# Rotary embedding of half a head: how the cosine and sine tables come into 128 partitions

## The chip, the cores and the metric

The kernel runs on one core of a Trainium2 chip. The time is device microseconds of one execution. Before the change it is 161.78 us, the median of three runs (161.61 to 161.86). A profile of one more execution has a span of 159.5 us from its first to its last instruction.

## What is computed

```
x: (16, 512, 16, 64) float32        batch, position, head, dimension
cos, sin: (512, 32) float32         position, half of the dimension

x1, x2 = x[..., :32], x[..., 32:]
first  = x1[..., :16] * cos[..., :16] - x1[..., 16:] * sin[..., :16]
second = x1[..., :16] * sin[..., :16] + x1[..., 16:] * cos[..., :16]
out    = concatenate([first, second, x2], axis=-1)
```

Only the first 32 of each head's 64 elements are turned; the other 32 pass through. Of each table's row, only the first 16 of 32 elements are used, and they serve all batches and heads. x and the output are 33.55 MB each, a table is 64 KB.

## The kernel before, in words

**Tiles.** x is read as one long array of rows, a row being one batch and position (16 heads of 64 elements, 4 KB). Four tiles (T = 4) of 128 partitions hold 16 rows (K = 16) in each partition, 64 KB a partition and 8.4 MB a tile. The buffer `ring` (line 45) holds three tiles, so tile 3 takes the place of tile 0. Since 16 rows of one batch follow each other in a partition, 512 positions fill 32 partitions (PB = 32), and the same pattern of positions repeats in each of the four groups of 32 partitions (REP = 4).

**Tables.** `table` (line 49) holds, for each partition, its 16 rows of cosine and of sine, the 16 used elements written twice in a row so that one multiply covers both halves of x1. So the four groups of 32 partitions hold the same content. It comes about in these steps:

- Line 61: DVE clears the used half of `stage`, in all 128 partitions.
- Lines 62 to 64: POOL issues one DMA for each table. Row j of 32 (16 positions, 2 KB) goes to partition 4j. The first of them waits for the clearing.
- Line 73: one stream shuffle on DVE. Within each group of 32 partitions, it brings the 8 rows that arrived there to 8 neighbouring places (repeated four times), in `spun`.
- Lines 78 to 80: four copies on DVE gather the groups' rows into partitions 0 to 31 of `packed`.
- Lines 82 to 86: four copies on DVE, one for each group of 32 partitions, write `table` from `packed`, each element twice.

**Loads, work and stores.** The functions `load` and `store` (lines 54 to 58) issue one DMA each, on SP's queue if nothing else is said. SP first issues the loads of tile 0, tile 1 and the second half of tile 2 (lines 65 to 67); they wait for nothing. `rotate(t, lo, hi)` (lines 90 to 103) does a part of a tile on DVE with four operations in place: x1 times sine into `b_t`, which lies in PSUM (line 96), x1 times cosine (97), a subtraction (98) and an addition (101). Tiles are done in halves of 8 rows, tile 2 in parts of 8, 5 and 3.

The order of the work is written by hand. After tile 0 is turned, SP issues its store, the load of the first half of tile 2, and the load of tile 3, which has to wait for the store of tile 0. The store of tile 1 is held back by a dependence written by hand (line 118) until the addition of the 5-row part of tile 2 is done. The store of tile 2 goes out on POOL's queue (line 116), the other stores on SP's.

Of the kernel before, what the change touches and what calls it, by code (L numbers as in the profile page):

```python
# [1 line left out]

# [4 lines left out]


@with_exitstack
def kernel(  # L10
    ctx: ExitStack,
    tc: tile.TileContext,
    x: bass.AP,
    cos: bass.AP,
    sin: bass.AP,
    out: bass.AP,
):
    nc = tc.nc
    fp32 = mybir.dt.float32
    P = 128  # L20
    B, S, H, D = x.shape
    Q = D // 4
    HF = D // 2

    K = 16
    T = B * S // (P * K)
    PB = S // K
    REP = P // PB  # L30
    R = H * D
    NS = 3
    KC = K // 2
    KM = 5

    xf = x.rearrange("b s h d -> (b s h d)").rearrange("(t p f) -> t p f", t=T, p=P)
    of = out.rearrange("b s h d -> (b s h d)").rearrange("(t p f) -> t p f", t=T, p=P)
    cosf = cos.rearrange("(p k) j -> p (k j)", k=K)
    sinf = sin.rearrange("(p k) j -> p (k j)", k=K)

    const_pool = ctx.enter_context(tc.tile_pool(name="const", bufs=1))
    b_pool = ctx.enter_context(tc.tile_pool(name="bp", bufs=1, space=bass.MemoryType.PSUM))


    ring = const_pool.tile([P, NS, K, H, D], fp32)
    stage = const_pool.tile([P, 2, K, HF], fp32)
    spun = const_pool.tile([P, 2 * K, Q], fp32)
    packed = const_pool.tile([PB, 2 * K, Q], fp32)
    table = const_pool.tile([P, 2, K, 2, Q], fp32)

    def rows(t, lo, hi):
        return ring[:, t % NS, lo:hi].rearrange("p k h d -> p (k h d)")

    def load(t, lo=0, hi=K):
        return nc.sync.dma_start(out=rows(t, lo, hi), in_=xf[t, :, lo * R : hi * R])

    def store(t, lo=0, hi=K, queue=nc.sync):
        return queue.dma_start(out=of[t, :, lo * R : hi * R], in_=rows(t, lo, hi))  # L58


    nc.vector.memset(stage[:, :, :, 0:Q], 0.0)  # L61
    spread = stage.rearrange("(j b) t k i -> j b t (k i)", b=REP)
    nc.gpsimd.dma_start(out=spread[:, 0, 0], in_=cosf)  # L63
    nc.gpsimd.dma_start(out=spread[:, 0, 1], in_=sinf)  # L64
    load(0)
    load(1)
    load(2, KC, K)

    PQ = PB // REP
    nc.vector.stream_shuffle(  # L73
        out=spun[:],
        in_=stage.rearrange("p t k j -> p (t k) j")[:, :, 0:Q],
        mask=[j % PQ * REP for j in range(PB)],
    )
    for q in reversed(range(REP)):
        n = PQ * (q + 1)
        nc.vector.tensor_copy(out=packed[0:n], in_=spun[q * PB : q * PB + n])  # L80

    for r in range(REP):
        nc.vector.tensor_copy(  # L83
            out=table[r * PB : (r + 1) * PB].rearrange("p t k c j -> p (t k) c j"),
            in_=packed.unsqueeze(2).to_broadcast((PB, 2 * K, 2, Q)),
        )
    C = table[:, 0].rearrange("p k c j -> p k (c j)")
    Sn = table[:, 1].rearrange("p k c j -> p k (c j)")

    def rotate(t, lo, hi):  # L90
        x1 = ring[:, t % NS, lo:hi, :, 0:HF]
        c = C[:, lo:hi].unsqueeze(2).to_broadcast((P, hi - lo, H, HF))
        s = Sn[:, lo:hi].unsqueeze(2).to_broadcast((P, hi - lo, H, HF))
        b_full = b_pool.tile([P, KC, H, HF], fp32, name="b_t")
        b_t = b_full[:, 0 : hi - lo]
        nc.vector.tensor_mul(out=b_t, in0=x1, in1=s)  # L96
        nc.vector.tensor_mul(out=x1, in0=x1, in1=c)  # L97
        nc.vector.tensor_sub(  # L98
            out=x1[:, :, :, 0:Q], in0=x1[:, :, :, 0:Q], in1=b_t[:, :, :, Q:HF]
        )  # L100
        return nc.vector.tensor_add(  # L101
            out=x1[:, :, :, Q:HF], in0=x1[:, :, :, Q:HF], in1=b_t[:, :, :, 0:Q]
        )

    rotate(0, 0, KC)
    rotate(0, KC, K)
    store(0)
    load(2, 0, KC)
    load(3)
    rotate(1, 0, KC)  # L110
    rotate(1, KC, K)
    behind_loads = store(1)
    rotate(2, KC, K)
    near = rotate(2, 0, KM)
    rotate(2, KM, KC)
    store(2, queue=nc.gpsimd)

    tc.add_manual_dep(
        behind_loads.ins,
        near.ins.name,  # L120
        mybir.DependencyInfo(mybir.DependencyClass.Sync, mybir.DependencyReason.DATA),
        reason="the store follows the loads at the DMA engines",
    )
    rotate(3, 0, KC)
    rotate(3, KC, K)
    store(3)


# [1 line left out]
_INS = ['x', 'cos', 'sin']  # L130
_OUTS = [((16, 512, 16, 64), 'float32')]


# [23 lines left out]
```

## Time and profile before

| | |
|---|---|
| Median of three runs | 161.78 us |
| Span of the profiled execution | 159.5 us |
| DVE busy | 112.9 us, 47 instructions |
| Moved by DMA | 67.24 MB, 422 GB/s over the span |
| Load of tile 0: issue, landing | 0.74 us, 22.94 us |
| DVE's first multiply starts | 23.03 us |
| DVE's last addition ends | 131.2 us |
| Issues of the stores of tiles 0, 1, 2, 3 | 49.92, 98.90, 104.62, 131.2 us |
| Landing of the last store, from its issue | 27.4 us |
| Cosine table: issue to landing | 9.0 us |
| Sine table: issue to landing | 13.3 us |

The span begins with the first instruction of the program and ends with the last; the time of a run has 2.3 us around it. The 16 DMA engines of the core serve two queues in this kernel: q1 holds what SP issues, q0 what POOL issues. A DMA into 128 partitions of 64 KB appears as 128 packets of 64 KB, 8 for each engine, and a small packet for each engine that signals the end. A DMA's instruction is short; what counts is when its data has landed, which other engines wait for. DVE is the vector engine, POOL is GpSimd, and a q behind an engine's name is its sequencer. In rows of the timeline, the first two numbers are start and duration, and a bracket tells how long the engine had been idle before and what ended that.

### The profile page before, as it was taken

How to read it: one execution, taken by the hardware profiler on the slowest of the kernel's cores; microseconds unless marked ns; L12 is line 12 of the kernel's file. 1: busy time of each engine (PE TensorE's matmuls, PEld its weight loads, DVE VectorE, ACT ScalarE, POOL GpSimd, SP SyncE). 2: the span in 40 equal slices, each digit the busy share in tenths (PEclk: the TensorE clock that was granted, in tenths of full speed). 3: DMA queues.
4: the chain of work that ended last, by engine and by line, in shares of the span. 5: the costliest groups of instructions: out<-in, count | busy, mean ns of one | idle time of the engine just before them, and what ended most of it. 6: DMA issues, size and time to landing. Idle time of an engine off the chain costs nothing.

```text
span 159.5 us, 115 instructions
## 1 busy us (share of the span) xinstructions
DVE 112.9 (71%) x47; POOL 1.9 (1%) x7
## 2 busy tenths in 40 slices
DVE  1000959999999999999999999999999990000000
POOL 3000000000000000000000000010000000000000
DMA  7969979799699699699996996996996997999966
GB/s 263 542 263 542 444 345 526 345 444 526 271 493 551 279 510 526 263 394 411 510 526 263 526 526 263 526 526 263 526 526 263 526 460 329 526 394 394 526 263 263
DMA packets 1360, 67.24 MB, mean 422 GB/s; under 512 B 176, under 2 KB 176, under 8 KB 208
## 3 DMA queue, kind: packets, MB, share of 16 engines
q1 hardware_dynamic: 1152, 58.72, 85.7%
q0 software_dynamic: 208, 8.52, 12.4%
HBM read 33.69 MB, written 33.55 MB: 422 GB/s over the span
## 4 chain that ended last, share of the span: by engine, by line
DVE 61%; DMA 14%; issue 5%; DVEq 1%
DVE b_t L96 22%; DVE ring L97 22%; DMA ring<-in_x_dram 14%; DVE ring L101 10%; DVE ring L98 7%; DVEq L152 1%; DVEq L96 0%
## 5 line engine op out<-in xcount | busy, mean ns | idle before, releaser
L96 DVE TENSOR_TENSOR b_t<-ring,table 128x4096 f32<-128x4096 f32 (+2 forms) x9 | 35.6, 3959 | 2.1 <-DMA ring<-in_x_dram 1.8
L97 DVE TENSOR_TENSOR ring<-ring,table 128x4096 f32<-128x4096 f32 (+2 forms) x9 | 35.5, 3950 | 0.3
L98 DVE TENSOR_TENSOR ring<-ring,b_t 128x2048 f32<-128x2048 f32 (+2 forms) x9 | 18.4, 2049 | 0.3
L101 DVE TENSOR_TENSOR ring<-ring,b_t 128x2048 f32<-128x2048 f32 (+2 forms) x9 | 18.4, 2043 | 0.0
L73 DVE LOAD_MASK_SELECT spun<-stage x1 | 0.0, 14 | 14.4 <-DMA stage<-in_sin_dram 14.4
L83 DVE COPY table<-packed 32x1024 f32<-32x1024 f32 x4 | 2.7, 684 | 0.1
L58 POOL DMA_DIRECT2D out_dram<-ring x1 | 0.6, 562 | 101.7 <-DVE ring L101 101.7
L80 DVE COPY packed<-spun 32x512 f32<-32x512 f32 (+3 forms) x4 | 1.7, 416 | 0.1
L61 DVE MEMSET stage<- 128x512 f32 x1 | 0.5, 485 | 0.9 <-PEq L141 0.9
L73 DVE STREAM_SHUFFLE spun<-stage 128x512 f32<-128x512 f32 x1 | 0.7, 721 | 0.0
L63 POOL DMA_DIRECT2D stage<-in_cos_dram x1 | 0.6, 644 | 1.3 <-DVE stage L61 1.3
L64 POOL DMA_DIRECT2D stage<-in_sin_dram x1 | 0.5, 535 | 0.0
L141 POOL MEMSET const-bfloat16-1.0<- 128x1 bf16 x1 | 0.1, 102 | 0.0
L141 POOL MEMSET const-float32-0.0<- 128x1 f32 x1 | 0.1, 99 | 0.2 <-issue 0.2
L141 POOL MEMSET const-float32-1.0<- 128x1 f32 x1 | 0.1, 99 | 0.0
L141 POOL MEMSET const-uint8-127<- 128x1 uint8 x1 | 0.1, 99 | 0.0
## 6 DMA issues: line engine op xcount, KB each, us to landing
ring<-in_x_dram SPq DMA_DIRECT2D x2, 4096.0 KB, 40.7
stage<-in_cos_dram POOLq DMA_DIRECT2D x1, 64.0 KB, 9.0
stage<-in_sin_dram POOLq DMA_DIRECT2D x1, 64.0 KB, 13.3
ring<-in_x_dram SPq DMA_DIRECT2D x3, 29.0
out_dram<-ring SPq DMA_DIRECT2D x3, 27.4
out_dram<-ring POOLq DMA_DIRECT2D x1, 39.5
```

Source lines behind the costliest of these rows:

```text
L58: return queue.dma_start(out=of[t, :, lo * R : hi * R], in_=rows(t, lo, hi))
L61: nc.vector.memset(stage[:, :, :, 0:Q], 0.0)
L63: nc.gpsimd.dma_start(out=spread[:, 0, 0], in_=cosf)
L64: nc.gpsimd.dma_start(out=spread[:, 0, 1], in_=sinf)
L73: nc.vector.stream_shuffle(out=spun[:], in_=stage.rearrange("p t k j -> p (t k) j")[:, :, 0:Q], mask=[j % PQ * REP for j in range(PB)],)
L80: nc.vector.tensor_copy(out=packed[0:n], in_=spun[q * PB : q * PB + n])
L83: nc.vector.tensor_copy(out=table[r * PB : (r + 1) * PB].rearrange("p t k c j -> p (t k) c j"), in_=packed.unsqueeze(2).to_broadcast((PB, ...
L96: nc.vector.tensor_mul(out=b_t, in0=x1, in1=s)
L97: nc.vector.tensor_mul(out=x1, in0=x1, in1=c)
L98: nc.vector.tensor_sub(out=x1[:, :, :, 0:Q], in0=x1[:, :, :, 0:Q], in1=b_t[:, :, :, Q:HF])
L101: return nc.vector.tensor_add(out=x1[:, :, :, Q:HF], in0=x1[:, :, :, Q:HF], in1=b_t[:, :, :, 0:Q])
L152: with _tile.TileContext(nc) as tc:
```

## The change

The tables now land in 32 neighbouring partitions, in the order in which they lie in memory, and the four copies into `table` read them from there, taking the first 16 of every 32 elements. The clearing of `stage`, the shuffle, the four packing copies and the two buffers between are gone; `stage` has 32 partitions instead of 128. The two table loads on POOL's queue now wait for no instruction. The four copies remain and write what they wrote. Loads and stores of x, the rotation and their order are the same.

```diff
-    stage = const_pool.tile([P, 2, K, HF], fp32)
-    spun = const_pool.tile([P, 2 * K, Q], fp32)
-    packed = const_pool.tile([PB, 2 * K, Q], fp32)
+    stage = const_pool.tile([PB, 2, K, HF], fp32)
     table = const_pool.tile([P, 2, K, 2, Q], fp32)
...
-    nc.vector.memset(stage[:, :, :, 0:Q], 0.0)
-    spread = stage.rearrange("(j b) t k i -> j b t (k i)", b=REP)
-    nc.gpsimd.dma_start(out=spread[:, 0, 0], in_=cosf)
-    nc.gpsimd.dma_start(out=spread[:, 0, 1], in_=sinf)
+    landed = stage.rearrange("p t k i -> p t (k i)")
+    nc.gpsimd.dma_start(out=landed[:, 0], in_=cosf)
+    nc.gpsimd.dma_start(out=landed[:, 1], in_=sinf)
     load(0)
     load(1)
     load(2, KC, K)
...
-    PQ = PB // REP
-    nc.vector.stream_shuffle(
-        out=spun[:],
-        in_=stage.rearrange("p t k j -> p (t k) j")[:, :, 0:Q],
-        mask=[j % PQ * REP for j in range(PB)],
-    )
-    for q in reversed(range(REP)):
-        n = PQ * (q + 1)
-        nc.vector.tensor_copy(out=packed[0:n], in_=spun[q * PB : q * PB + n])
-
+    half = stage.rearrange("p t k j -> p (t k) j")[:, :, 0:Q]
     for r in range(REP):
         nc.vector.tensor_copy(
             out=table[r * PB : (r + 1) * PB].rearrange("p t k c j -> p (t k) c j"),
-            in_=packed.unsqueeze(2).to_broadcast((PB, 2 * K, 2, Q)),
+            in_=half.unsqueeze(2).to_broadcast((PB, 2 * K, 2, Q)),
         )
```

## The prediction

> **What bounds the kernel now.** I read the busy times first, then the DMA queues, the chain of waits, the timeline of the first 24 us, and last the traffic in a few short windows.
>
> ```profile
> span 159.5 us, 115 instructions
> DVE 112.9 (71%) x47; POOL 1.9 (1%) x7
> q1 hardware_dynamic: 1152, 58.72, 85.7%
> q0 software_dynamic: 208, 8.52, 12.4%
> ```
>
> The queue rows give packets, MB and the share of the engines' time. The two queues' packets take 85.7 + 12.4 = 98.1% of the time of all 16 DMA engines. That is 156.5 us of 159.5, so about 3 us per engine are free. A view by stretches says where:
>
> ```profile
> 0.00:1.70 1.70, 0.48 (x1) 0.20 (x4) 1.00 0.00 0
> 1.70:23.00 21.30, 5.13 (x10) 1.18 (x2) 1.00 1.07 449
> 50.00:100.00 50.00, 49.59 (x17) 0.00 (x0) 1.00 1.02 436
> 131.00:158.00 27.00, 0.21 (x1) 0.00 (x0) 1.00 0.99 427
> 158.00:160.00 2.00, 0.00 (x0) 0.00 (x0) 1.00 0.00 0
> ```
>
> The columns are the stretch, its length, DVE and POOL busy, the clock, the DMA share and GB/s (packets count where they start, so a share can pass 1). Nothing moves before 1.7 us, nothing after 158; between them the engines are never short of work. So the time is: 1.7 us until the first packet, the engines' own work, 1.3 us until the end is noticed. DVE is the second, nearly equal bound: from 23.03 to 131.2 us it never waits, and it starts when tile 0 has landed. The timeline of the start:
>
> ```profile
> 0.74 1.33 SPq L55 DMA_DIRECT2D ring<-in_x_dram  x3
> 0.92 0.48 DVE L61 MEMSET stage<- 128x512 f32 x1 [0.92 <-PEq L141]
> 1.71 0.64 POOL L63 DMA_DIRECT2D stage<-in_cos_dram  x1 [1.26 <-DVE stage L61]
> 2.35 0.54 POOL L64 DMA_DIRECT2D stage<-in_sin_dram  x1
> 15.83 0.01 DVE L73 LOAD_MASK_SELECT spun<-stage  x1 [14.43 <-DMA stage<-in_sin_dram]
> 15.86 0.72 DVE L73 STREAM_SHUFFLE spun<-stage 128x512 f32<-128x512 f32 x1
> 16.61 1.76 DVE L80 COPY packed<-spun 32x512 f32<-32x512 f32 x4
> 18.41 2.78 DVE L83 COPY table<-packed 32x1024 f32<-32x1024 f32 x4
> 23.03 4.43 DVE L96 TENSOR_TENSOR b_t<-ring,table 128x4096 f32<-128x4096 f32 x1 [1.85 <-DMA ring<-in_x_dram]
> ```
>
> The last line is the one that decides most: the table was ready at 18.41 + 2.78 = 21.19 us, and DVE then sat 1.85 us idle until the load of tile 0 (issued 0.74, landed 22.94). The 14.43 us wait for the sine table looks large and costs nothing.
>
> **The change part by part.**
>
> *DVE work removed.* The memset (0.48), the shuffle with its mask (0.72 + 0.01) and the four packing copies (1.76): 2.98 us of instructions. The stretch from 15.83 to 18.41, 2.58 us, goes from between the tables' landing and the four copies. All of it ends before 22.94, so it only lengthens the wait: with the sine table landing at 15.7 as before, the table is ready at 15.8 + 2.8 = 18.6 and the wait grows to 4.4 us. Gain 0. What covers it is the load of tile 0.
>
> *The four copies stay, with another source.* They read 16 of every 32 elements instead of a packed row. No row shows a copy from such a source. Lower bound: the same 684 ns each. Upper bound: the rate of DVE's long multiplies, which read two tensors, 4433 ns for 4096 elements: 1.08 ns by 1024 elements = 1.11 us each, 4.5 us in all. I take 0.7 us, since the same instruction and output stay. Even 4.5 us after 15.8 ends at 20.3, 2.6 us ahead of the tile. Cost 0 at both ends.
>
> *The table loads move.* POOL's wait for the memset (1.26 us in the row) goes. POOL has no other work: its last start-up step in the trace is a semaphore at 0.6 us. So the cosine issue starts between 0.65 and 0.92 us (when DVE gets its own first instruction), 0.8 to 1.1 us earlier; it ends at about 1.3 to 1.6, the sine issue at 1.8 to 2.1. Nothing is queued behind them on POOL until the store at 104.62 us, which waits for DVE. SP's queue is not touched: its three loads go out at 0.74 either way. What meets what at the DMA engines is new, though. In the trace the first packets of x run from 1.75 us, and the tables come in between:
>
> ```profile
> DMA packets 32, 1.11 MB, mean 1114 GB/s; under 512 B 0, under 2 KB 0, under 8 KB 16
> q1 hardware_dynamic: 16, 1.05, 241.8%
> q0 software_dynamic: 16, 0.07, 15.9%
> ```
>
> This is the traffic from 7 to 8 us: 16 packets of 4 KB, the cosine table, one for each engine. They take 15.9% of 16 engines' 1 us, 0.159 us an engine; the window from 12 to 13 us says the same of the sine table. The tables are therefore 2 x 0.159 = 0.32 us of an engine that has no free time afterwards, and this is the only term through which the change reaches the end. Lower bound of the move: both tables run before x's first packet, in the empty 1.7 us, a gain of 0.32. Upper bound: they only change places with x packets, gain 0, since the sum on an engine is the same. The sine issue begins at 1.3 us at the earliest, and the one clean start in the trace, SP's first load, takes 1.0 us from issue (0.74) to first packet (1.75). So the sine table cannot be in the empty time; the cosine table, issued at 0.65 to 0.92, would arrive at 1.66 to 1.93, on the edge. I take half of the cosine table: -0.08 us.
>
> [...]
>
> *The tables land elsewhere.* Before, the 32 rows of 2 KB of each table go to every fourth partition, over all 128. Now they go to partitions 0 to 31. The bytes and rows are the same; no row of the trace shows a load into 32 neighbouring partitions. Lower bound: nothing changes, each engine carries 4 KB of each table: 0. Upper bound: if the landing place narrows the traffic to half of the engines, or to half of the ways into the memory, that half has four 4 KB packets' time instead of two: +0.32 us, and the slowest engine ends the kernel. I take the middle, +0.16 us, because the 16 equal packets speak for an even deal and the destination against.
>
> [...]
>
> *Sum.* DVE 0; copies 0; earlier issue -0.08; landing place +0.16: +0.08 us. Against the profiled execution, 159.5 us of span becomes 159.6. The runs' median is 161.78, 2.3 us more than the profiled span, which nothing here changes. Forecast 161.86, I write 161.9. By its bounds (-0.16 to +0.32) the forecast's own range is 161.6 to 162.1. A measurement can tell about 0.2%, 0.32 us, from no change: 161.46 to 162.10.
>
> **The rivals.**
>
> *The narrow landing costs more: slower.* Place: the table packets among the first rounds of x loads. Here half of the engines carry both tables (+0.32), and x packets bound for the same places wait as long again (+0.32): +0.32 to +0.64, so 162.1 to 162.4, middle 162.25. For it: the DMA engines are full from 1.7 to 158 us, so nothing absorbs it; store 0 is issued at 49.92, just as the first loads run out, so DVE cannot make it up. Against: 131 KB among 67 MB, and 16 even packets before. It decides from the point where one engine's extra is over 0.32 us.
>
> *The empty start is used: faster.* Both tables run before or inside the fill of x's first packets, -0.32: 161.46, and down to 161.3 if tile 0 also lands with less disturbance. For it: 1.7 us in which nothing moves, and POOL free at 0.6. Against: the sine issue can't begin before 1.3.
>
> *The tables come late, or nothing moves earlier.* If x's packets crowd them out, the sine table could land after 22.94 - 2.8 = 20.1 us; from there each us delays DVE, and store 0 with it, 1 to 1. It landed at 15.7 when issued later, so I give this little. That POOL is held by something else and issues at 1.7 as before belongs to the forecast: 161.8 to 162.1.
>
> **How the numbers follow.** Forecast 0.45, narrow landing 0.31, empty start 0.20, late tables 0.04 (163 or more). Same is the forecast, 0.45; slower is the narrow landing and the late tables, 0.35; faster is the empty start, 0.20. The range runs from 161.4 to 162.4: it takes in most of both rivals and leaves out the start's lower end, the narrow landing's last part and the late tables, together 0.2.
>
> **What would show it.** Right: no shuffle; POOL's first issue near 0.7 us; the table ready before 19 us, and the wait of line 96's first multiply on tile 0 grown from 1.85 to 4 us or more, while it still starts within 0.2 us of 23.03; the DMA queues' shares again 98% together. The landing term is read from the 4 KB packets: 16 for each table, 0.159 us an engine, or fewer and longer. The start term is read from whether any 4 KB packet precedes 1.75 us. The forecast is wrong if the end of the last packet moves by more than 0.32 us from 158.2, if tile 0 lands elsewhere than 22.94 by as much, or if the engines show gaps between 23 and 158 us.

## The result and the profile after

The kernel after takes 162.86 us in the median of four runs (162.39 to 163.25); the kernel before beside it took 161.69 us (161.47 to 161.86). The ratio is 1.0075, with a 95% interval of 1.0052 to 1.0099: slower by some 1.2 us, clear of the 0.2% that a measurement can tell, and outside the forecast range of 161.4 to 162.4. The profiled execution is the fastest of the four, 162.39 us with a span of 160.6; its gap to the span of before is 1.1 us. The four spans are 160.6, 161.0, 161.2 and 161.5 us, so that in the median the span grew by 1.5 us or a little more (before: 159.5 to 159.6 in the median of each later series). The time grew by less, because 1.75 to 1.79 us lie around the span after the change and 2.0 to 2.1, in the median, before it.

From the page's first lines and queue rows, for the kernel after:

```profile
span 160.6 us, 108 instructions
DVE 110.0 (68%) x40; POOL 1.9 (1%) x7
q1 hardware_dynamic: 1152, 58.72, 85.7%
q0 software_dynamic: 208, 8.52, 12.3%
```

DVE does 2.9 us less, as worked out. The packets and bytes are the same, and the queues' shares are the same, of a longer span: the same bytes took about 1 us more of every engine. The timeline of the start, kernel after:

```profile
0.74 1.32 SPq L53 DMA_DIRECT2D ring<-in_x_dram  x3
1.26 0.63 POOL L60 DMA_DIRECT2D stage<-in_cos_dram  x1 [0.82 <-PEq L140]
1.89 0.51 POOL L61 DMA_DIRECT2D stage<-in_sin_dram  x1
16.44 2.77 DVE L71 COPY table<-stage 32x1024 f32<-32x1024 f32 x4 [16.44 <-DMA stage<-in_sin_dram]
23.69 4.43 DVE L84 TENSOR_TENSOR b_t<-ring,table 128x4096 f32<-128x4096 f32 x1 [4.48 <-DMA ring<-in_x_dram]
```

The table loads go out 0.45 us earlier than before (1.26 against 1.71) and the sine table is nevertheless used 0.6 us later (16.44 against 15.83). The copies still cost 2.77 us, and DVE's wait for tile 0 has grown from 1.85 to 4.48 us: DVE has nothing to do with the loss. But tile 0 itself is 0.66 us late (23.69 against 23.03). Where that comes from is seen in the traffic of the 1 us in which the cosine packets go out, kernel after:

```profile
q1 hardware_dynamic: 16, 1.05, 266.0%
q0 software_dynamic: 16, 0.07, 15.9%
```

and in the 1 us of the sine packets (12.2 to 13.2 us), kernel after:

```profile
q1 hardware_dynamic: 16, 1.05, 278.1%
q0 software_dynamic: 16, 0.07, 18.5%
```

Sixteen packets of 64 KB that take 266.0% of 16 engines' 1 us take 2.66 us each; the same packets took 241.8%, 2.42 us, before. All sixteen are alike: 2.65 to 2.68 us behind the cosine table, 2.71 to 2.83 behind the sine table. So each table still has 16 packets, one for each engine, and they still look cheap, 0.159 and 0.185 us. The cost lies on the x packet that follows them on each engine: +0.24 us behind the cosine table, +0.36 behind the sine table, together with the 0.03 on the sine packets 0.63 us.

The rest of the 1.1 us appears near 70 us, at what is called the turn from here on: the last 64 KB packets of tile 0's store (on SP's queue from 49.92 us in the kernel before, from 50.58 in the kernel after) and the first packets of the load behind it. The store's last packets, in the kernel before (67.7 to 68.7 us):

```profile
q1 hardware_dynamic: 16, 1.05, 276.4%
```

and in the kernel after (68.5 to 69.5 us):

```profile
q1 hardware_dynamic: 16, 1.05, 306.3%
```

Even in the kernel before, this packet takes 2.76 us instead of 2.42; in the kernel after, it takes 3.06. To set such stretches side by side I take, for a stretch of the profile, its length less the time that the bytes moved in it need at 65,536 bytes in 2.418 us per engine: the time lost per engine. These are computed from the trace's packet records, in us. "Mean end" is when the sixteen last 64 KB packets end, in the mean; "behind" is how much later than this mean the last of them ends:

```
kernel                  5.2-24 us   24-66    66-80 (turn)   98-157   mean end   behind
before                     0.00     -0.04       0.43         -0.02     158.07     0.15
after                      0.65      0.04       0.83         -0.09     159.13     0.22
```

Two losses, then: 0.65 us while the tables come in (the local loss from here on) and 0.40 us more at the turn; the engines' mean end is 1.06 us later.

### The profile page after: what moved, and what is told of

Its sections match the earlier page's. It is cut to its first block, busy times and chain, and to the rows that moved or that the text cites. A ratio compares the mean times of both kernels' runs of the same rounds, so it can differ in the third digit from the quotient of the medians.

```text
span 160.6 us, 108 instructions
## 1 busy us (share of the span) xinstructions
DVE 110.0 (68%) x40; POOL 1.9 (1%) x7
## 3 DMA queue, kind: packets, MB, share of 16 engines
q1 hardware_dynamic: 1152, 58.72, 85.7%
q0 software_dynamic: 208, 8.52, 12.3%
## 4 chain that ended last, share of the span: by engine, by line
DVE 61%; DMA 14%; issue 5%; DVEq 1%
DVE b_t L84 22%; DVE ring L85 22%; DMA ring<-in_x_dram 14%; DVE ring L89 10%; DVE ring L86 7%; DVEq L140 1%; DVEq L84 0%
## 5 line engine op out<-in xcount | busy, mean ns | idle before, releaser
L71 DVE COPY table<-stage 32x1024 f32<-32x1024 f32 x4 | 2.7, 684 | 16.5 <-DMA stage<-in_sin_dram 16.4
```

The costliest lines, as they stand in the source:

```text
L71: nc.vector.tensor_copy(out=table[r * PB : (r + 1) * PB].rearrange("p t k c j -> p (t k) c j"), in_=half.unsqueeze(2).to_broadcast((PB, 2 ...
```

## The experiments

Four to twelve executions of each kernel were timed beside the kernel before, at 161.5 to 161.6 us. Lost times are one profiled execution's. A table load into 32 neighbouring partitions is called narrow, one into every fourth of the 128 spread; "..." in an edit stands for lines left out. Two theories stood at the start: that the landing place does the harm (rows converging on 32 neighbouring partitions), or that the earlier issue does. Where an experiment fills the tables with a constant, its transfers are what is studied.

### The wait put back

```diff
+    nc.vector.memset(stage[:, :, :, 0:Q], 0.0)
     landed = stage.rearrange("p t k i -> p t (k i)")
```

> The kernel after, with one thing put back: DVE clears the used half of the 32-partition buffer first, so the table loads wait as they did before. Theory of the landing place (rows that converge on 32 neighbouring partitions hold up the x packet behind them): still slow, 162.6 to 163.0 us, the first x packet after each table 2.6 to 2.8 us long instead of 2.42, tile 0 landing near 23.6. Theory of the timing (the earlier, unhindered issue does the harm): back to 161.6 to 161.9, those packets 2.42, tile 0 landing near 22.95.

It took 163.09 us (162.91 to 163.87), ratio 1.0104 (1.0085 to 1.0124), with the issue back at 1.69 us. The x packets behind the cosine table, in a window of 1 us of this kernel:

```profile
q1 hardware_dynamic: 16, 1.05, 256.7%
```

2.57 us each, and 2.69 behind the sine table; tile 0 is used at 23.66. With the wait back the loss is still there, so the missing wait is not what causes it.

### The old landing place without the wait

```diff
-    nc.gpsimd.dma_start(out=landed[:, 0], in_=cosf)
-    nc.gpsimd.dma_start(out=landed[:, 1], in_=sinf)
...
+    nc.vector.memset(stage[:], 0.5)
+    spread = wide.rearrange("(j b) t k i -> j b t (k i)", b=REP)
+    nc.gpsimd.dma_start(out=spread[:, 0, 0], in_=cosf)
+    nc.gpsimd.dma_start(out=spread[:, 0, 1], in_=sinf)
```

> The tables land in every fourth partition again, without a wait, and are not used: the cosine and sine tables are filled with a constant by DVE, so the output's rotated half is not the reference's. Theory of the landing place: as before, 161.4 to 161.8 us, x packets behind the tables 2.42 us. Theory of the timing: as after, 162.6 to 163.0. A gain below 161.4 would say that the earlier issue alone is worth something.

161.36 us (161.18 to 161.53), ratio 0.9987 (0.9978 to 0.9995). The 1 us of the cosine packets in this kernel:

```profile
q1 hardware_dynamic: 16, 1.05, 241.8%
q0 software_dynamic: 16, 0.07, 15.9%
```

No x packet is stretched, and the early issue is harmless. This kernel differs from after in one thing more, that nothing waits for its tables; the run with every second partition, below, differs from it in the landing place alone. The small gain is not one of the transfers: the median span is 159.6 us, that of before, and only the time around it is shorter (1.78 us). A second program with these transfers (below) came out at 161.55.

### No table loads

```diff
-    nc.gpsimd.dma_start(out=landed[:, 0], in_=cosf)
-    nc.gpsimd.dma_start(out=landed[:, 1], in_=sinf)
+    nc.vector.memset(stage[:], 0.5)
```

> The table loads are left out and the tables filled with a constant, so the output's rotated half is not the reference's. It prices the tables whole: before has them at 0.32 us by the packets' own time, so 161.3 to 161.5 here, and 1.3 to 1.6 us under after, by the theory of the landing place. If the loss of some 0.3 to 0.4 us at the turn from the store of tile 0 to the next loads (70 us) has nothing to do with the tables, it appears here as well, x packets there 3.0 us in the mean against 2.76 before, and the time is 161.6 to 161.9. By the theory of the timing the tables cost no more than 0.32 wherever they land: 161.3 to 161.5 too.

160.95 us (160.82 to 161.09), ratio 0.9958 (0.9946 to 0.9970). The kernel before takes 0.6 us more, but only 0.4 of it in the span (159.6 us in the median against 159.2), near the tables' own 0.32; the rest lies around the span, which is 1.79 us here. Against this kernel, with the same time around the span, the spread tables of the run above cost 0.4 us and the narrow ones of the kernel after 1.9 (162.86 less 160.95, from different series). The turn loses 0.49 us here, about what it loses before, so the dearer turn of after is not something that every kernel of this kind has.

### The tables on the Activation engine's queue

```diff
-    nc.gpsimd.dma_start(out=landed[:, 0], in_=cosf)
-    nc.gpsimd.dma_start(out=landed[:, 1], in_=sinf)
+    nc.scalar.dma_start(out=landed[:, 0], in_=cosf)
+    nc.scalar.dma_start(out=landed[:, 1], in_=sinf)
```

> The kernel after, with both table loads issued on the Activation engine's queue, which is empty, instead of POOL's. They should go out near 0.75 us and meet the first x packets near 1.8. Theory of the landing place: where the table packets come while x packets are under way, they hold them up as in after, 162.6 to 163.0; if they slip ahead of the first x packets, most of the stretch is gone and it is 161.4 to 161.9. Theory of the timing: earlier still is no better, 162.6 or more.

163.76 us (162.79 to 164.24), ratio 1.0124 (1.0100 to 1.0148). Issued at 0.74 us, the first rows still come behind the first x packet, in pieces of 2 KB at 4.9, 7.4, 12.4 and 15.2 us, and the x packets behind them take 2.43, 2.49, 2.79 and 2.56 us. Lost until 24 us: 0.64, as in after. This neither hides the tables nor makes them cheaper, and POOL's queue is not needed for the loss.

### Every second partition of the lower half

```diff
...
+    spread = wide[0 : 2 * PB].rearrange("(j b) t k i -> j b t (k i)", b=2)
+    nc.gpsimd.dma_start(out=spread[:, 0, 0], in_=cosf)
+    nc.gpsimd.dma_start(out=spread[:, 0, 1], in_=sinf)
```

> The tables land in every second partition of the lower half (0, 2 to 62), without a wait, and are not used: the tables are filled with a constant, so the output's rotated half is not the reference's. [...] Theory of the crowding of neighbours (what hurts is that rows of different engines lie side by side): between, 161.6 to 162.2, packets 2.45 to 2.55.

163.08 us (162.63 to 164.46), ratio 1.0106 (1.0073 to 1.0138); lost until 24 us: 0.63, and 0.98 at the turn. From 7 to 8 us of this kernel, fifteen of the sixteen x packets behind the cosine table start:

```profile
q1 hardware_dynamic: 15, 0.98, 246.4%
```

They take 2.63 us each. Twice the room between the rows helps nothing: partitions 0 to 62 by twos cost what 0 to 31 cost (0.63 us lost until 24 us against 0.65), and every fourth partition up to 124 stretches no packet (0.00). Between these two runs nothing but the landing place differs, neither the issue, nor the buffers, nor who waits for the tables: 163.08 us against 161.36.

### Meant to be late, but was not

A clearing of one element per table after tile 1 is turned was to hold back narrow table loads until 77 us. The program placed the clearing at 1.87 us instead, so the loads went out at 2.25.

```diff
...
+    nc.vector.memset(late[:, :, 0, 0:1], 0.0)
+    later = late.rearrange("p t k i -> p t (k i)")
+    nc.gpsimd.dma_start(out=later[:, 0], in_=cosf)
+    nc.gpsimd.dma_start(out=later[:, 1], in_=sinf)
```

> The table loads land in 32 neighbouring partitions but only after tile 1 is turned, near 77 us, and are not used: the tables are filled with a constant, so the output's rotated half is not the reference's. The narrow loads then come behind the turn from stores to loads at 70 us. Theory that the second loss, at that turn, is a consequence of the narrow loads before it: only the local loss remains, some 0.6 to 0.9 us on the 160.95 of the kernel without tables, so 161.5 to 161.9, and the turn costs what it costs without tables (0.4 to 0.5 us over two full and two half packets). Theory that a narrow landing costs its whole 1.9 us wherever it lies, or that the turn is independent of it: 162.4 to 163.0.

163.69 us (162.42 to 163.92), ratio 1.0110 (1.0082 to 1.0139). What was expected was not tried. The run is another early narrow landing, with 0.43 us lost until 24 us and 1.00 at the turn, and since nobody reads these rows, the harm is in the transfers and not in what uses them.

### All 128 partitions with 512 bytes each

```diff
-    cosf = cos.rearrange("(p k) j -> p (k j)", k=K)
+    cosf = cos.rearrange("(p k) j -> p (k j)", k=K // REP)
...
+    for b in range(REP):
+        for c in range(2):
+            nc.vector.stream_shuffle(
+                out=spun_b[:, c, b],
+                in_=stage[:, c, :, 0:Q],
+                mask=[j % PQ * REP + b for j in range(PB)],
+            )
```

> A version meant to be better than both: each table lands in all 128 partitions, 4 positions or 512 bytes in each, so nothing has to be cleared and the loads wait for nothing; eight small shuffles in place of one bring the rows together, the packing and the four copies are as before. Theory of the landing place: x packets stay at 2.42 us, the time is that of before or a little less, 161.2 to 161.7. If 512-byte rows cost the engines more than 2 KB rows, each table's packets take 0.2 to 0.4 us an engine instead of 0.159 and it is 161.7 to 162.2. Theory that spreading only helps with few rows: 162.5 or more.

162.66 us (162.29 to 163.28), ratio 1.0076 (1.0058 to 1.0094): a miss of the theory as I had it. The x packets are not stretched (241.8% in the window of the cosine packets), 0.02 us is lost until 24 us, and the engines' mean end is 158.36, 0.3 us later than before. But one engine ends 0.83 us behind the mean in the profiled execution.

### Each table twice

```diff
...
+    second = again.rearrange("p t k i -> p t (k i)")
+    nc.gpsimd.dma_start(out=second[:, 0], in_=cosf)
+    nc.gpsimd.dma_start(out=second[:, 1], in_=sinf)
```

> The kernel after with each table loaded twice into 32 neighbouring partitions; the second pair is not used and the output is the reference's. Theory of the landing place: four x packets are stretched by 0.24 to 0.36 us instead of two, and each table has its own 0.16 besides, so tile 0 lands near 24.6 to 24.9 and the time is 163.4 to 164.2. Theory that it is a single disturbance, which the first table sets off: 162.8 to 163.2.

163.49 us (162.96 to 163.63), ratio 1.0108 (1.0090 to 1.0126). All four x packets are stretched (2.59, 2.74, 2.74 and 2.72 us) and tile 0 is used at 24.81 instead of 23.69. So the local loss comes once for each narrow load: 1.28 us in all, 0.99 until 24 us and 0.29 behind that, about twice that of after. The time did not follow in full, since the turn cost only 0.69 us here.

### A cover for the turn

In three kernels (before, after, and the one with 512-byte rows) the load of tile 2's first half was moved to POOL's queue, issued at 63.5 to 64.8 us:

```diff
...
-    load(2, 0, KC)
     load(3)
-    rotate(1, 0, KC)
+    half_done = rotate(1, 0, KC)
+    cover = load(2, 0, KC, queue=nc.gpsimd)
+    tc.add_manual_dep(
+        cover.ins,
+        half_done.ins.name,
...
```

> The kernel before, with the load of the first half of tile 2 moved from SP's queue to POOL's, issued when the first half of tile 1 is turned (near 63 us), so that its packets lie beside the last packets of tile 0's store. Theory that the second loss lies at that turn, where each engine has nothing but the store's last packet and then a cold load: the 0.4 us that before loses there (over two full and two half packets) goes, 161.0 to 161.3 us. Theory that the turn is harmless and the engines' work alone counts: 161.5.

> The kernel after with the same cover. Theory of two losses (the local one, some 0.6 us until tile 0 lands, and a second at the turn, 0.4 to 1.3 us with engines that fall behind): only the first remains, 161.6 to 162.0, and 0.5 to 0.7 us over the covered kernel before. Theory of one loss whose later part is made up of small delays everywhere, or of a turn that hits wherever the queue changes: 162.4 to 163.0.

> The kernel with 512-byte rows in all 128 partitions (loads wait for nothing) with the same cover. It had no loss until tile 0 landed but was at 162.66. Theory of two losses: its loss was all at the turn, so it comes to the covered kernel before, 161.0 to 161.4. Else, if 512-byte rows cost something that the packets do not show: 162.2 or more.

162.55, 163.68 and 164.12 us, with ratios of 1.0066 (1.0052 to 1.0080), 1.0138 (1.0120 to 1.0157) and 1.0162 (1.0143 to 1.0181): all three slower than without the cover. In the covered kernel before, the turn still loses 0.46 us, tile 0's store now ends later, the load of tile 3 is issued at 72.85 instead of 71.72 us, and a new loss of 0.70 us appears after 98 us. So the cover was none, and these runs don't test the two losses. The difference of the first two, 1.13 us, is near that of before and after, but not made up in the same way: the covered kernel after loses 1.02 us until 24 us, with table loads like those of after (0.65), and 0.83 at the turn. The covered 512-byte kernel loses 1.06 at the turn without any narrow load.

### Narrow, but after the turn

The same intent as the one that went out early, now with a dependence written by hand; the loads go out at 76.96 us.

```diff
...
+    for part, src in ((0, cosf), (1, sinf)):
+        came = nc.gpsimd.dma_start(out=later[:, part], in_=src)
+        tc.add_manual_dep(
+            came.ins,
+            turned.ins.name,
...
```

> The table loads into 32 neighbouring partitions, not used and not early: they are issued when tile 1 is turned, near 77 us, after the turn; the tables are filled with a constant, so the output's rotated half is not the reference's. Theory that narrow loads early make the turn dearer: the turn costs what it costs without tables (0.4 to 0.5 us), only the local loss comes on top of 160.95: 161.5 to 161.9. Theory that the turn's cost has nothing to do with the tables before it: turn 0.4 to 1.0 at random, 161.5 to 163.

162.19 us (162.00 to 162.53), ratio 1.0044 (1.0031 to 1.0058), 1.24 us over the kernel without tables. Nothing is lost until 66 us, 0.70 at the turn, and 0.90 between 80 and 98 us, where the tables now come in. So narrow loads cost time here too, without a tile that waits for them and far from the start. No engine ends over 0.17 us behind the mean. The 0.70 at the turn, with no table load ahead of it, shows that the turn varies by itself.

### Is it a chance of the program?

```diff
...
+    for i in range(8):
+        nc.vector.memset(idle[:, i], 0.0)
     C = table[:, 0].rearrange("p k c j -> p k (c j)")
```

> The kernel before with eight small clearings of an unused buffer on DVE before the first rotation, while DVE waits for tile 0 anyway; transfers are untouched. Theory that the transfers set the time: 161.3 to 161.9, the turn at 70 us costs 0.4 to 0.7 us over two full and two half packets. Theory of a chance of each program (another program, other places, another cost at the turn): may lie anywhere from 161.0 to 163.0, and a move by over 0.5 us speaks for it.

> The kernel after with the same eight idle clearings. Theory that the transfers set the time: 162.5 to 163.3, turn 0.8 to 1.0 us, one or two engines behind the others at the end by 0.2 to 1.5 us. Theory of a chance of each program: may be at 162.0 to 162.3 (the local loss alone) or anywhere above.

The kernel before with these idle clearings took 161.98 us (161.81 to 162.04), ratio 1.0025 (1.0016 to 1.0034), the kernel after with them 163.44 (163.11 to 163.74), ratio 1.0115 (1.0096 to 1.0134). So another program with the same transfers can differ by 0.4 us, and less than that can't be put down to an edit here. In the span the first of them is even 0.7 us longer (160.2 us in the median against 159.5), with 0.3 us less around it. The gap between the landing places stays: 1.46 us between these two, 1.15 of it in the median spans.

### Half the dose, and another narrow load

```diff
...
-    nc.gpsimd.dma_start(out=landed[:, 1], in_=sinf)
+    spread = wide.rearrange("(j b) k i -> j b (k i)", b=REP)
+    nc.gpsimd.dma_start(out=spread[:, 0], in_=sinf)
```

> The cosine table lands in 32 neighbouring partitions, the sine table in every fourth one and is not used (its part of the table is a constant, so the output's rotated half is not the reference's). Half the dose: the x packet behind the cosine table 2.55 to 2.68 us, the one behind the sine table 2.42, tile 0 near 23.3. Theory that local loss and turn both follow the narrow bytes: 162.0 to 162.5. Theory that the turn's loss is all or nothing: 162.5 or more. Theory that only the local loss is the landing's: 161.6 to 161.8.

162.67 us in the median, but with runs from 161.63 to 163.97 and one of 164.46 that the ratio of 1.0058 (1.0034 to 1.0081) leaves out. The two windows of 1 us with the cosine and with the sine packets of this kernel say which table hurts:

```profile
q1 hardware_dynamic: 16, 1.05, 255.6%
...
q1 hardware_dynamic: 16, 1.05, 243.1%
```

2.56 us behind the table in neighbouring partitions, 2.43 behind the spread one, in one and the same execution.

```diff
...
+    eighth = wide.rearrange("(e r) f -> e r f", r=16)
+    rows8 = xf[0].rearrange("(e r) f -> e r f", r=16)
+    nc.gpsimd.dma_start(out=eighth[:, 0], in_=rows8[:, 0, 0:1792])
```

> No table loads (tables filled with a constant, so the output's rotated half is not the reference's); instead one early load of 8 rows of 7 KB from x into every sixteenth partition of an unused buffer, one row for each of 8 engines, 0.26 us on each of them. Theory that any early disturbance of the engines' step makes the turn dearer: turn 0.7 to 1.0 us, engines behind by 0.5 or more, 161.8 to 162.8. Theory that it takes a narrow landing: turn 0.4 to 0.6, and 160.95 plus at most 0.3, so 161.0 to 161.3.

162.51 us (161.97 to 163.82), ratio 1.0076 (1.0047 to 1.0104). All 16 x packets behind this load were stretched, to 2.70 us, though only 8 rows came in, and the turn lost 0.85. It was meant as a load that is not narrow, and behaved as one that is; it tells nothing of a disturbance without narrowness. Eight rows 16 partitions apart are few places too.

### Spread loads in other programs

The spread transfers without a wait were run once more with the eight idle clearings, and the 512-byte transfers without their shuffles:

```diff
...
+    whole = wide.rearrange("p t k i -> p t (k i)")
+    nc.gpsimd.dma_start(out=whole[:, 0], in_=cosf)
+    nc.gpsimd.dma_start(out=whole[:, 1], in_=sinf)
```

> e2 (tables in every fourth partition, no wait, not used; tables filled with a constant, so the output's rotated half is not the reference's) with eight idle clearings of an unused buffer. Theory that the landing place sets the time: 161.2 to 162.0 (p1 showed that another program can be 0.4 us off), runs within 0.6 us of each other. Theory that e2 was a lucky program: 162.3 or more.

> The transfers of f3 (each table in all 128 partitions, 512 bytes in each, no wait), not used; tables filled with a constant, so the output's rotated half is not the reference's, and no shuffles. Theory that f3's loss came with its transfers: 162.3 to 163.0, engines behind the others by 0.5 us or more. Theory that it was that program's: 161.2 to 162.0.

161.55 us (161.38 to 161.77), ratio 1.0003 (0.9995 to 1.0012), for the rows in every fourth partition: the landing place holds in a second program, and the early issue gains nothing. 162.45 us for the 512-byte rows, with runs from 161.54 to 162.90, ratio 1.0043 (1.0022 to 1.0064): most of that kernel's loss came with its transfers, though they stretch no packet.

### The kernels side by side

Computed from the packet records as above, us per engine:

```
kernel                      5.2-24 us  66-80 (turn)  mean end  behind  median us
before                         0.00        0.43       158.07     0.15    161.6
before, idle clearings         0.00        0.52       158.17     0.66    161.98
every fourth, no wait          0.00        0.67       158.24     0.15    161.36
the same, idle clearings       0.00        0.55       158.11     0.19    161.55
no tables                     -0.01        0.49       157.80     0.15    160.95
neighbours at 77 us           -0.01        0.70       159.15     0.17    162.19
128 x 512 bytes, unused        0.02        0.45       158.22     1.25    162.45
128 x 512 bytes                0.02        0.53       158.36     0.83    162.66
cosine alone in neighbours     0.17        0.48       158.37     0.77    162.67
neighbours (after)             0.65        0.83       159.13     0.22    162.86
neighbours, idle clearings     0.55        0.95       159.06     0.75    163.44
neighbours, with the wait      0.47        1.00       159.20     0.77    163.09
neighbours, Activation queue   0.64        0.96       159.34     1.51    163.76
neighbours, each twice         0.99        0.69       159.92     0.56    163.49
every second of the lower 64   0.63        0.98       159.22     1.05    163.08
neighbours, nobody reads       0.43        1.00       159.09     1.70    163.69
8 rows of 7 KB, no tables      0.30        0.85       158.66     0.31    162.51
```

The first column sorts the kernels cleanly by landing place, although its size is not fixed: two narrow tables cost 0.43 to 0.65 us in it, and 1.02 in the covered kernel after. The turn is dearer in most kernels with early narrow loads (0.69 to 1.00, but 0.48 with the cosine alone) than in those without (0.43 to 0.70, but 1.06 in the covered 512-byte kernel). And the column "behind" is a third thing: an engine that ends later than the others. The records don't name the engine of a packet; it is followed from packet to packet, each starting where the last one ended. With the exception of the kernel before with idle clearings, and of a part in the kernel on the Activation queue, such engines fall behind at the turn: in the unused 512-byte kernel the last of the 16 is 0.19 us behind the median at 68.3 us, 1.01 at 72.2 and 1.36 at the end. Every engine has the same work (followed in this way, 56 packets of 64 KB and 16 of 32 KB on each in before and in after), and what that one lost at the turn it did not make up by the end; the kernel ends with the last engine. It fits with the wide scatter of some of these kernels' runs, up to 2.3 us, where those of before lie 0.7 us apart; that the scatter comes from there is not shown, since one execution of each was profiled.

## Why the prediction was wrong

**What bounds the kernel: right.** But for the first packets and the turn, the engines are full to the end (85.7 + 12.3 = 98.0% of the span after), and what they lost came out in the span of the profiled pair almost one to one: +1.06 us in their mean end, +1.1 in the span.

**DVE work removed, copies kept: right.** Gain 0 and cost 0. The copies took 683 ns against 684, and the wait for tile 0 grew to 4.48 us as said; with the sine table landing late, the table was ready at 19.2 instead of 18.6.

**Earlier issue: right in effect, off in time.** POOL issued at 1.26 us, not at 0.65 to 0.92; the bracket of its row names a wait of 0.82 us for a start-up step (PEq L140), where the row of before named the memset. No table packet came before x's first, and the term of -0.08 is nothing that the runs show: without the wait and with the old landing the median span is 159.6 us in two programs, that of before.

**The tables land elsewhere: the step that failed, by its bounds.** I took +0.16 us between 0 and +0.32, "if the landing place narrows the traffic to half of the engines, or to half of the ways into the memory, that half has four 4 KB packets' time instead of two", and the rival with +0.32 to +0.64 was the dearer form of the same. The sign was right, and the rival named the place: x packets wait behind the tables. But the price was made from the table packets' own 0.159 us, on half of the engines. It is not in them, which stayed at 0.159 and 0.185 us and sixteen in number. It is in the next 64 KB packet of every engine, 0.24 and 0.36 us longer, 0.63 in all with the 0.03 of the sine packets. That this meets the upper end of the rival, 0.64, is luck: neither of the two halves from which the rival was made, both tables on half of the engines and the same wait again for x, is what happened, and other programs with such loads lost from 0.43 to 1.02 us.

**What no step had: the turn.** It stood in the sum at nothing. The prediction read the stretches as full and let them pass; the 0.43 us lost between 66 and 80 us in the kernel before lies within a share near 1 and was not seen. After the change it is 0.83, and engines fall behind there. Together with the local loss this is the whole 1.1 us between the profiled spans. The other three runs of after, with spans 0.4 to 0.9 us longer, were not profiled. An engine that is behind could account for them, as one is 0.75 and 0.77 us behind in two other kernels with these loads, but this is not shown.

**The time around the span: taken as fixed, and it was not.** The sum went from the span to the time by 2.3 us "which nothing here changes", a difference between two executions. Where one execution has both numbers, 1.72 to 2.22 us lie around the span of the kernel before, 2.0 to 2.1 in the median of each series, and 1.75 to 1.79 around that of after. So some 0.3 us came back outside the span, and the change cost 1.5 us in the span where the time says 1.2. What sets it is open: the kernel after with idle clearings has 2.1 again.

**What is not settled.** That a narrow landing makes the kernel slower, and causes the first loss, is shown: two kernels that differ in the landing place alone (163.08 and 161.36 us), one table narrow and one spread in the same execution, the wait put back, the doubled dose, the late loads. Why the packet behind it is stretched is not shown, nor is what way its bytes take into the memory, which the bound reckoned with. That it makes the turn dearer is likely and no more: the two groups overlap (0.48 and 0.70), and one program differs from another by 0.4 us. Why an engine falls behind at the turn, and why 512-byte rows that stretch nothing bring this about as well, stays open. The covers that were to take the turn away did not. No version was found that beats the kernel before by more than programs differ.

## What to carry to other kernels

Where the DMA engines are full, look at where a small load lands and not only at its bytes: 131 KB in 32 neighbouring partitions cost 1.9 us here and 0.4 us in every fourth partition, and some 0.6 us of the 1.9 stands on the packets right behind the loads. A stretch whose share of the engines reads near 1 can still hide a loss of 0.4 us (66 to 80 us reads 0.93 before, with 0.43 lost, and 1.01 after, with 0.83); compare bytes moved with the full rate (here 2.418 us for 64 KB on an engine) before calling it full. The time around the span can move by 0.3 us as well, so compare spans as well as times. An edit that takes away instructions and waits which other work covers gained nothing here (2.9 us of DVE work went and the wait for tile 0 grew from 1.85 to 4.48 us), so what was left of it was its side effects.

## What the runs showed that I had not expected

- Rows in every second partition of 0 to 62 cost the same as in 0 to 31 (0.63 and 0.65 us lost), every fourth partition of all 128 nothing (0.00).
- Eight rows of 7 KB to eight partitions stretched the following 64 KB packet on all 16 engines, to 2.70 us from 2.42.
- The last packets of a store that is followed by loads on the same queue take 2.76 (before) to 3.13 us (after, with idle clearings) in the mean instead of 2.42, and in the unused 512-byte kernel one engine lost some 0.8 us there that it did not make up.
- Eight small DVE instructions that change no transfer moved the time by 0.25% (0.16 to 0.34), and the median span by 0.7 us.
